# A decoder layer on one core: a prologue that runs shift and scale two block pairs ahead, an end without accumulating transfers, and side work visited by planned lag

## The chip, the core and the metric

The kernel runs on one core of a Trainium2 chip. The metric is the device time of one execution in microseconds (us). Engine names are those of the profile: PE is the tensor engine (PEld its weight loads), DVE the vector engine, ACT the scalar engine, POOL the GpSimd engine, and SP the queue from which most transfers are issued.

## What is computed

One layer of a decoder trunk for 1024 prompt tokens and 32 sample tokens (8 sequences of 4), model width 1024. The reference, cut to what matters:

```python
mod = silu(c) @ w_ada + b_ada                      # c: one row for the prompt, one per sample sequence
sh1, sc1, gt1, sh2, sc2, gt2 = split(mod, 6)
h = rmsnorm(x, g_pre_mix) * (1 + sc1) + sh1
z = h @ w_in                                       # 24 blocks of 128 columns
ya = chunk_gmlp(z...); yb = hgrn2(z...); yc = conformer_conv(z...)
y = concat(ya, yb, yc) @ w_out
x = x + gt1 * rmsnorm(y, g_post_mix)
h = rmsnorm(x, g_pre_mlp) * (1 + sc2) + sh2
y = square(relu(h @ w_up)) @ w_down
x = x + gt2 * rmsnorm(y, g_post_mlp)
```

Everything is float32. Large products are made from three products of a faster 32-bit matmul type: each operand is split into a rounded high part (`hi`) and the rest (`lo`), and hi·hi + hi·lo + lo·hi is accumulated.

## The kernel before

**Tiling.** Features lie on the 128 partitions. The 1056 tokens are cut into three token groups c = 0, 1, 2 of 352; the last 32 tokens of group 2 are the samples, whose shift and scale differ by sequence. The 1024 input features are 8 blocks k, kept in three tiles per group (blocks 0-2, 3-5, 6-7: the table `KK`). One output block of one group is 8 blocks x 3 matmuls of 128x128 by 128x352, summed in one PSUM bank.

**Prologue (lines 148-690).** The inputs `x` are loaded, squared on ACT (`first_squares`), folded over the blocks on DVE (`fold_first`), summed over the partitions on PE (`token_sums`), and turned into 1/rms per token (`token_rms`, `diagonal`, `by_feature`, `rstd_copy`). `scale_x` multiplies x by it, partly on DVE and partly on POOL. Shift and scale (`mod`, `G1`) come from `w_ada`, two blocks k at a time: 4 transfers (`ada_load`), 32 small matmuls (`ada_first`), a copy (`ada_copy`), and a transpose with the bias added (`ada_turn`). `first_h` makes hi and lo of h for one block and all groups. `first_blocks` goes over k and adds the products of the first two output blocks m = 0, 1 of all three groups in six banks; for a pair of blocks k it makes h, then issues the products, and between them the shift and scale of the next pair. `warm` issues matmuls of zeros. Behind the loop both blocks are evacuated, and the main part begins with the next output block (`in_block`).

**Main part.** Products follow a fixed order (`ORDER`, then `w_out`, `w_up`, `w_down`). Everything else (convolution taps on DVE, the recurrence, norms, the remaining shift and scale in `ada(q)`) is written as generators. `step(t)`, called between groups of matmuls, advances a planner's clock and visits generators whose due time has come while the planned load of the engines (`credit`) allows. A `yield 9.0` puts the next visit at least 9 planned us later. The visits decide only where instructions stand in each engine's queue; on the chip every engine goes through its queue in order.

**Norm between the halves.** `after_mix` (line 1361) scales one group, adds the input by an accumulating transfer from POOL's queue, stores the sum (`x1d`), waits 6.0, squares, sums and normalises again, and makes hi and lo for `w_up`.

**End.** The last product `w_down` goes over token groups `GROUPS`: group 2; then group 0 with 96 tokens of group 1; then the last 256 tokens of group 1. Behind each, `after_ff` (line 1475) scales by 1/rms. For the first two, `x1d` is added by accumulating transfers from POOL's queue and `out_yT` is then written from SP's; of the second, the last tile's part (kk = 2) is put off until the last group's sums are out. For the last group, `x1` lies in SBUF and DVE adds it.

Of the kernel before, what the change touches and what calls it, by code (L numbers as in the profile page):

```python
# [37 lines left out]
class Metered:  # L38
# [5 lines left out]
    def __getattr__(self, op):  # L44
        f = getattr(self._eng, op)

        def call(**kw):
# [5 lines left out]
            return f(**kw)  # L53

        return call
# [38 lines left out]
def trunk_kernel(ctx: ExitStack, tc: tile.TileContext, xT, cT, wada0, wada, vec, cst, msk, win, wout, wup,  # L94
# [245 lines left out]
    def ada(q):  # L340
        ps = bank("adaps")

        for k in range(8):
# [2 lines left out]
            raws = [e("rawada") for h2 in range(2)]
            for h2 in range(2):
                SP.dma_start(out=raws[h2][:, 0:1024], in_=wada[q - 1, k, h2])
            yield 7.0
            for j in range(4):  # L350
                PE.matmul(out=ps[32 * j:32 * j + 32, :], lhsT=scT[:, k, :],
                          rhs=raws[j // 2][:, (j % 2) * 512:(j % 2) * 512 + 512],
                          start=(k == 0), stop=(k == 7), skip_group_check=True)
            drop(2)
# [195 lines left out]
    def load_first(b):  # L550

        a = ada_load(b)
        rows = {0: slice(0, 2), 2: slice(2, 4), 4: slice(4, 8)}.get(b)
        if rows:
            for src, raw in raw_first:
                SP.dma_start(out=raw[:, rows, :], in_=src[:, rows, :])
        return a, rows
# [9 lines left out]
    x_s = mp.tile([128, 8, NS], F32, tag="s0", name="x_s")

    def first_squares(c):
        for kk, (k0, n) in enumerate(KK):  # L570
            ACT.activation(out=sqs[c][:, k0:k0 + n, :], in_=xs_in[c](kk), func=AF.Square)

    def fold_first(c, part):
        sq = sqs[c]
        for a, b, n in (((0, 3, 3),), ((0, 1, 1), (0, 2, 1), (6, 7, 1), (0, 6, 1)))[part]:
            DVE.tensor_tensor(out=sq[:, a:a + n, :], in0=sq[:, a:a + n, :], in1=sq[:, b:b + n, :], op=ALU.add)

    def rstd_copy(c, d):
        ps = by_feature(d)
        ACT.copy(out=rstds[c], in_=ps)  # L580

    def scale_x(c, eng, kk, a, b):

        w = CW if c < 2 else CW - NS
        t = xs_in[c](kk)[:, a:b, 0:w]
        eng.tensor_tensor(out=t, in0=t, in1=rep(rstds[c][:, 0:w], b - a), op=ALU.mult)

    G1 = cp.tile([128, 8, 9], F32, name="G1")
    for c in range(2):
        first_squares(c)  # L590
        fold_first(c, 0)
        fold_first(c, 1)
# [21 lines left out]
    scale_x(0, DVE, 0, 0, 2)
    fold_first(2, 1)
    rstd_copy(1, dg1)
    scale_x(1, POOL, 0, 2, 3)
    scale_x(1, POOL, 1, 0, 3)
    scale_x(1, DVE, 0, 0, 2)
    warm(3)  # L620
    (raw_ada, rows0) = ada_raws.pop(0)
    ada_0 = ada_first(raw_ada, 4)
    for i in range(2):
        next(ada_0)
    sums2 = token_sums(sqs[2][:, 0, :])
    rt2 = token_rms(sums2)
    dg2 = diagonal(rt2)
    next(ada_0)
    copied = ada_copy(next(ada_0))
    rstd_copy(2, dg2)  # L630
# [2 lines left out]
    warm(4)
    for kk, (k0, n) in enumerate(KK):
        POOL.tensor_copy(out=x_s[:, k0:k0 + n, :], in_=xs_in[2](kk)[:, :, CW - NS:])
    POOL.tensor_tensor(out=x_s, in0=x_s, in1=rep(rstds[2][:, CW - NS:], 8), op=ALU.mult)
    scale_x(2, POOL, 0, 2, 3)
    scale_x(2, POOL, 1, 0, 3)
    for c in range(NCH):
        scale_x(c, POOL, 2, 0, 2)  # L640
    h = [(hc(f"h{c}hi"), hc(f"h{c}lo")) for c in range(NCH)]
    sh1 = mod[:, 0:8, :]

    def first_h(k, cs=range(NCH)):

        ops = []
        for c in cs:
            w = CW if c < 2 else CW - NS
            u = xs_in[c](k // 3)[:, k % 3, 0:w]
            hi, lo = h[c][0][:, k, 0:w], h[c][1][:, k, 0:w]  # L650
            DVE.tensor_scalar(out=u, in0=u, scalar1=G1[:, k, 0:1], scalar2=sh1[:, k, 0:1], op0=ALU.mult, op1=ALU.add)
            ACT.copy(out=r(hi), in_=u)
            ops.append((u, hi, lo))
        for u, hi, lo in ops:
            DVE.tensor_tensor(out=r(lo), in0=u, in1=hi, op=ALU.subtract)

    def first_h_sample(k, n):

        u = x_s[:, k:k + n, :]
        hi, lo = h[2][0][:, k:k + n, CW - NS:], h[2][1][:, k:k + n, CW - NS:]  # L660
        DVE.tensor_tensor(out=b4(u), in0=b4(u), in1=seqs(G1[:, k:k + n, :]), op=ALU.mult)
        DVE.tensor_tensor(out=b4(u), in0=b4(u), in1=seqs(sh1[:, k:k + n, :]), op=ALU.add)
        ACT.copy(out=r(hi), in_=u)
        DVE.tensor_tensor(out=r(lo), in0=u, in1=hi, op=ALU.subtract)

    def first_blocks(evacs):

        pss = [[pm_tile() for c in range(NCH)], [pb.tile([128, CW], F32, tag="b", name="pmt2") for c in range(NCH)]]

        def products(k, c):  # L670
            xh, xl = (x[:, k, :] for x in h[c])
            for part, x in ((0, xh), (1, xh), (0, xl)):
                for m in range(2):
                    nc.tensor.matmul(out=pss[m][c], lhsT=r(w_first[m][part][:, k, :]), rhs=r(x),  # L674
                                     start=(k == 0 and part == 0 and x is xh), stop=(k == 7 and x is xl))

        for k in range(0, 8, 2):
            if k == 0:
                first_h(0, (0, 1))
                scale_x(2, DVE, 0, 0, 2)  # L680
                first_h(0, (2,))
            else:
                first_h(k)
            first_h_sample(k, 2)
            first_h(k + 1)
            if ada_raws and ada_raws[0][1]:
                split_first(ada_raws[0][1])
            for c in range(NCH):
                products(k, c)
            if k < 6:  # L690
                copied = ada_copy(next(ada_first(ada_raws.pop(0)[0])))
            if k < 4:
                ada_raws.append(load_first(k + 4))
            products(k + 1, 0)
            if k < 6:
                ada_turn(copied)
            products(k + 1, 1)
            products(k + 1, 2)
# [973 lines left out]
```

## Time and profile before

| | us |
|---|---|
| median of 3 runs (lowest, highest) | 1289.9 (1286.49, 1290.26) |
| the profiled execution, its own time | 1287.62 |
| its span, first to last instruction | 1285.9 |
| PE busy | 1239.1 (96%) |
| DVE busy | 743.7 (58%) |
| ACT busy | 474.4 (37%) |
| POOL busy | 112.7 (9%) |

The granted PE clock over the span is 0.981 of full. A row of a timeline or of the chain of waits gives start, duration and instruction; "x3" at its end merges three instructions; in brackets stands the idle time ahead of it and what ended it. A row of groups gives busy time, mean ns of one, and the idle time ahead. Rows of windows give busy time and count for PE, PEld, DVE, ACT and POOL, then the granted clock, the busy share of the transfer engines, and GB/s. Most operations are recorded on one helper line (L53), so groups are told apart by tiles.

### The profile page before, as it was taken

The numbers are of one execution on the slowest core, as the hardware profiler recorded it, in microseconds if no ns is written. First come the engines' busy times: TensorE is split into PE (matmuls) and PEld (weight loads), VectorE is DVE, ScalarE is ACT, GpSimd is POOL, SyncE is SP. The second block draws the span as 40 slices with busy tenths as digits, with TensorE's granted clock in tenths as the row PEclk, the third lists the DMA queues.
The fourth block names the chain that finished last, engine by engine and source line by source line (L and its number), as shares of the span: only waits on it lengthen the run. The fifth ranks groups of instructions, "written<-read, shape, count | busy, mean of one in ns | idle before, by whom it ended". The sixth has DMA issues, their size and how long they took to land.

```text
span 1285.9 us, 20903 instructions
## 1 busy us (share of the span) xinstructions
PE 1239.1 (96%) x8794; PEld 1196.8 (93%) x8794; DVE 743.7 (58%) x1206; ACT 474.4 (37%) x890; POOL 112.7 (9%) x135
## 2 busy tenths in 40 slices
PE   7799999999999999999999999999999999999994
PEld 6688898889999989999999999999999999999994
DVE  6888889986768758864333333333333333333365
ACT  4332464536674655655320320321311311312343
POOL 3300020302110133210000000000000000000002
PEclk7799999999999999999999999999999999999997
DMA  8446324310111364443211111111111111111218
GB/s 321 148 169 188 108 93 164 108 42 18 63 43 55 119 201 121 151 124 118 79 50 50 47 38 48 50 50 49 35 49 50 50 38 45 50 50 41 71 24 214
DMA packets 39376, 113.41 MB, mean 88 GB/s; under 512 B 10209, under 2 KB 12161, under 8 KB 39153
## 3 DMA queue, kind: packets, MB, share of 16 engines
q1 hardware_dynamic: 34544, 98.92, 22.5%
q0 software_dynamic: 4736, 13.14, 4.5%
q8 instruction: 69, 1.13, 0.3%
q14 instruction: 27, 0.21, 0.0%
HBM read 101.91 MB, written 10.14 MB: 87 GB/s over the span
## 4 chain that ended last, share of the span: by engine, by line
PE 86%; DVE 6%; ACT 3%; DMA 2%; issue 1%; POOL 1%; SPq 0%; ACTq 0%; DVEq 0%
PE pmt L53 78%; PE pmt L674 2%; PE adaps L53 2%; DVE sq L53 1%; PE sc L53 1%; DVE acc L53 1%; DMA rawada<-in_wada 1%; DMA o<-in_xT 1%; PE us L53 1%; DVE o L53 1%; PE stps L53 1%; PE ob L53 1%; DMA x<-in_xT 1%; ACT sq L53 1%; DVE x L53 0%
## 5 line engine op out<-in xcount | busy, mean ns | idle before, releaser
L53 PE MATMUL pmt<-ah,whi 128*128 128x352 f32 (+2 forms) x744 | 241.3, 324 | 0.8 <-ACT acc L53 0.8
L53 PE MATMUL pmt<-al,whi 128*128 128x352 f32 (+2 forms) x744 | 240.4, 323 | 0.3 <-DVE al L53 0.2
L53 PE MATMUL pmt<-ah,wlo 128*128 128x352 f32 (+2 forms) x744 | 240.3, 323 | 0.0
L53 ACT CAST whi<-raw 128x1024 fp32r<-128x1024 f32 (+2 forms) x114 | 115.2, 1014 | 261.9 <-PE pmt L53 259.4
L53 DVE TENSOR_TENSOR acc<-acc,pmt 128x352 f32<-128x352 f32 (+2 forms) x176 | 87.8, 502 | 167.9 <-PE pmt L53 167.9
L53 DVE TENSOR_TENSOR wlo<-raw,whi 128x1024 fp32r<-128x1024 f32 (+2 forms) x114 | 139.5, 1227 | 58.4 <-ACT whi L53 57.8
L53 DVE TENSOR_TENSOR rsq<-relu 128x352 f32<-128x352 f32 x84 | 44.1, 525 | 189.2 <-ACT relu L53 189.2
L53 PEld LDWEIGHTS pmt<-ah,whi 128*128 128x128 f32 x744 | 139.8, 188 | 2.2 <-ACT acc L53 1.0
L53 PEld LDWEIGHTS pmt<-al,whi 128*128 128x128 f32 x744 | 140.1, 188 | 1.6 <-DVE al L53 0.8
L53 PEld LDWEIGHTS pmt<-ah,wlo 128*128 128x128 f32 x744 | 139.9, 188 | 0.4
L53 ACT ACTIVATE relu<-pmt 128x352 f32<-128x352 f32 x96 | 44.5, 464 | 234.8 <-PE pmt L53 234.8
L53 PE MATMUL pmt<-h22hi,wlo 128*128 128x352 f32 x256 | 82.6, 323 | 0.0
L53 PE MATMUL pmt<-h22hi,whi 128*128 128x352 f32 x256 | 82.5, 322 | 0.0
L53 PE MATMUL pmt<-h22lo,whi 128*128 128x352 f32 x256 | 82.4, 322 | 0.0
L53 DVE SCALAR_TENSOR_TENSOR cva<-cvx,vec_t,cva 128x1024 f32<-128x1024 f32 x60 | 76.5, 1276 | 0.0
L53 PE MATMUL pmt<-h21hi,whi 128*128 128x352 f32 x232 | 75.1, 324 | 0.0
L53 PE MATMUL pmt<-h21hi,wlo 128*128 128x352 f32 x232 | 74.9, 323 | 0.0
L53 PE MATMUL pmt<-h20hi,wlo 128*128 128x352 f32 x232 | 74.9, 323 | 0.0
L53 PE MATMUL pmt<-h20hi,whi 128*128 128x352 f32 x232 | 74.8, 322 | 0.0
L53 PE MATMUL pmt<-h20lo,whi 128*128 128x352 f32 x232 | 74.7, 322 | 0.0
L53 PE MATMUL pmt<-h21lo,whi 128*128 128x352 f32 x232 | 74.7, 322 | 0.0
L1482 POOL DMA_DIRECT2D acc<-x1d x3 | 2.6, 877 | 699.6 <-DVE acc L53 689.5
(352 smaller groups left out, 2800.2 us busy)
## 6 DMA issues: line engine op xcount, KB each, us to landing
rawada<-in_wada SPq DMA_DIRECT2D x48, 512.0 KB, 6.2
raw<-in_wup SPq DMA_DIRECT2D x36, 512.0 KB, 3.4
raw<-in_wdn SPq DMA_DIRECT2D x36, 512.0 KB, 3.4
raw<-in_win SPq DMA_DIRECT2D x22, 512.0 KB, 3.6
raw<-in_wout SPq DMA_DIRECT2D x20, 512.0 KB, 3.6
x<-in_xT SPq DMA_DIRECT2D x6, 528.0 KB, 7.2
o<-in_xT POOLq DMA_DIRECT2D x6, 528.0 KB, 6.1
x1d<-o POOLq DMA_DIRECT2D x6, 528.0 KB, 7.3
```

The source lines that it names most:

```text
L53: return f(**kw)
L674: nc.tensor.matmul(out=pss[m][c], lhsT=r(w_first[m][part][:, k, :]), rhs=r(x), start=(k == 0 and part == 0 and x is xh), stop=(k == 7 and ...
L1482: POOL.dma_start(out=src(kk), in_=x1d[2][:, k0:k0 + n, :], accum_op=ALU.add)
```

## The change

1. **Prologue.** `x` is loaded in the order of groups 2, 0, 1. The constants one, epsilon and zero are set on POOL instead of loaded. Squares are no longer folded: PE multiplies each squared block by a matrix of ones, so that the sum appears on all partitions (21 matmuls of 352 columns; of group 1 DVE first adds one pair per tile), and 1/rms is one square root and one reciprocal of 128x352. POOL does no arithmetic on x. For groups 0 and 1 one DVE instruction applies 1/rms and scale, ACT adds the shift while it rounds hi, and DVE forms lo; for group 2 DVE applies 1/rms ahead (`scale_x`), and ACT scale and shift. Shift and scale of the first two pairs are made before the first product, h of pair p+1 during the products of pair p, and those of pair p+2 behind the products of its first block. The products of the last block k = 7 are issued per output bank, each followed by its evacuation. The weights of the next output block get a place of their own (`homes[2]`) and are split inside the loop.
2. **Paced visits.** Seven waits of generators change: five become `settle(extra, engines)`, a fixed part plus the planned backlog of the named engines (POOL is now planned too); `after_mix` waits 14.0 instead of 6.0; `ada(q)` takes two blocks at a time and waits 11.0 instead of 7.0 for one.
3. **End.** The tile kk = 2 of group 0 (with its 96 tokens of group 1) is no longer added by accumulating transfers: `x1d` of group 0, blocks 6-7, is loaded to SBUF (`x1_last`) and DVE adds both parts. The other accumulating transfers stay.

The diff, cut:

```diff
-    warm(30)
-    sums = [token_sums(sqs[0][:, 0, :])]
...
-    scale_x(0, POOL, 0, 2, 3)
-    scale_x(0, POOL, 1, 0, 3)
...
+    def first_squares(c, kk, added):
...
+        ACT.activation(out=sq[:, k0:k0 + n, :], in_=xs_in[c](kk), func=AF.Square)
+        if added:
+            DVE.tensor_tensor(out=sq[:, k0, :], in0=sq[:, k0, :], in1=sq[:, k0 + 1, :], op=ALU.add)
+        for k in range(k0, k0 + n):
+            if not added or k != k0 + 1:
+                PE.matmul(out=sums[c], lhsT=ones, rhs=sq[:, k, :], start=k == 0, stop=k == (6 if added else 7))
+
+    def first_rstd(c):
+        ACT.activation(out=rstds[c], in_=sums.pop(c), func=AF.Sqrt, scale=1.0 / 1024, bias=eps)
+        DVE.reciprocal(out=rstds[c], in_=rstds[c])
...
+        def plain(c):
+            ts = [(xs_in[c](kk)[:, a + i, :], k + i) for kk, a, b, k in spans(p) for i in range(b - a)]
+            for t, k in ts:
+                DVE.scalar_tensor_tensor(out=t, in0=t, scalar=G1[:, k, 0:1], in1=rstds[c], op0=ALU.mult,
+                                         op1=ALU.mult)
+                ACT.activation(out=r(h[c][0][:, k, :]), in_=t, func=AF.Identity, bias=sh1[:, k, 0:1], scale=1.0)
+            for t, k in ts:
+                DVE.scalar_tensor_tensor(out=r(h[c][1][:, k, :]), in0=t, scalar=sh1[:, k, 0:1],
+                                         in1=h[c][0][:, k, :], op0=ALU.add, op1=ALU.subtract)
...
+        plain(0)
+        last()
+        plain(1)
+        last_lo()
...
+    for i in range(3):
+        next(parts)
+        warm(2)
...
+    ada_turn(copied)
...
+    first_h(0)
+    scale_x(2, 1)
+    for at in ada_first(ada_raws.pop(0)):
+        warm(2)
+    copied = [ada_copy(at)]
+    ada_raws.append(ada_load(6))
...
+        for p in range(4):
+            k = 2 * p
+            both(0, k)
+            if p < 3:
+                ada_turn(copied.pop())
+                first_h(p + 1)
+                if p < 2:
+                    scale_x(2, p + 2)
+                    split_first(slice(2 * p + 2, (4, 8)[p]))
+                else:
+                    split_next()
             else:
...
+                ACT.copy(out=r(means), in_=cst_t[:, K_BLK:K_BLK + 256])
+            both(2, k)
+            both(1, k)
+            if p < 2:
+                for at in ada_first(ada_raws.pop(0)):
+                    pass
+                copied.append(ada_copy(at))
+            if p < 3:
+                for c in (0, 2, 1):
+                    both(c, k + 1)
...
+    def settle(extra, *keys):
+
+        return extra + max(0.0, *(-credit[k] for k in keys))
...
-        yield 9.0
+        yield settle(5.0, "act", "pool")
...
-        yield 3.0
+        yield settle(3.0, "act", "pool")
         drop()
         add_task("norm" if p < 3 else "last", head_norm(p, st, oo, sq, hi, lo))
...
-        yield 6.0
+        yield 14.0
         for d in sum_squares(src, box):
...
-                if last:
-                    DVE.tensor_tensor(out=y, in0=y, in1=x1[:, k0:k0 + n, a:b], op=ALU.add)
+                if kk < 2 and not last:
+                    POOL.dma_start(out=y, in_=x1d[c][:, k0:k0 + n, a:b], accum_op=ALU.add)
+                    SP.dma_start(out=yT[c, :, k0:k0 + n, a:b], in_=y)
                 else:
-                    POOL.dma_start(out=y, in_=x1d[c][:, k0:k0 + n, a:b], accum_op=ALU.add)
+                    rest.append((y, c, k0, n, a, b))
```

Where the instructions stand, at three places. First PE's queue behind the fillers (`pmt<-d`, products of zeros). `adaps` are the small matmuls of shift and scale for one pair, `adapt` the transpose that releases it, `h0hi` the high part of h of group 0. Before:

```order
L53 MATMUL pmt<-d_83 128x128 x3
L53 MATMUL adaps<-rawada,scT 32x128 x16
L53 MATMUL sums<-cst_t,sq_151 88x1 x4
L53 MATMUL adaps<-rawada,scT 32x128 x16
L53 MATMUL stps<-diag,cst_t 128x352
L53 MATMUL adapt<-cst_t,adasb 128x128
L53 MATMUL pmt<-d_83 128x128 x4
L674 MATMUL pmt<-h0hi,whi 128x352
```

After, from the first pair's transpose on:

```order
L56 MATMUL adapt<-cst_t,adasb 128x128
L56 MATMUL adaps<-rawada,scT 32x128 x8
L56 MATMUL pmt<-d_83 128x128 x2
L56 MATMUL adaps<-rawada,scT 32x128 x8
L56 MATMUL pmt<-d_83 128x128 x2
L56 MATMUL adaps<-rawada,scT 32x128 x8
L56 MATMUL pmt<-d_83 128x128 x2
L56 MATMUL adaps<-rawada,scT 32x128 x8
L56 MATMUL pmt<-d_83 128x128 x2
L673 MATMUL pmt<-h0hi,whi 128x352
```

The round of the second pair, 32 matmuls with eight fillers between them, now stands ahead of the first product; the sums of squares (`sums` and `stps` before) are all further ahead.

Second, DVE's queue from the moment that scale (`G`) of the first pair is known; `x_0_129` is group 0's tile of blocks 0-2 in the change. Before:

```order
L53 TENSOR_TENSOR mod<-adapt,vec_t 128x2x18
L53 SCALAR_TENSOR_TENSOR G_156<-mod,vec_t 128x18
L53 TENSOR_TENSOR wlo<-raw,whi 128x256 x2
L53 TENSOR_SCALAR x_0_105<-x_0_105,G_156,mod 128x352
L53 TENSOR_SCALAR x_0_111<-x_0_111,G_156,mod 128x352
L53 TENSOR_TENSOR h0lo<-x_0_105,h0hi 128x352
L53 TENSOR_TENSOR h1lo<-x_0_111,h1hi 128x352
L53 TENSOR_TENSOR x_0_117<-x_0_117,rstd 128x2x320
```

After:

```order
L56 TENSOR_TENSOR mod<-adapt,vec_t 128x2x18
L56 SCALAR_TENSOR_TENSOR G_154<-mod,vec_t 128x18
L56 SCALAR_TENSOR_TENSOR x_1_131<-x_1_131,G_154,rstd 128x352 x2
L56 SCALAR_TENSOR_TENSOR h0lo<-x_1_131,mod,h0hi 128x352 x2
L56 TENSOR_TENSOR x_1_125<-x_1_125,G_154 128x2x32
L56 TENSOR_TENSOR x_1_125<-x_1_125,mod 128x2x32
L56 SCALAR_TENSOR_TENSOR x_1_137<-x_1_137,G_154,rstd 128x352 x2
L56 SCALAR_TENSOR_TENSOR h1lo<-x_1_137,mod,h1hi 128x352 x2
L56 TENSOR_TENSOR h2lo<-x_1_125,h2hi 128x704
L56 TENSOR_TENSOR x_2_127<-x_2_127,rstd 128x704
L56 TENSOR_TENSOR wlo<-raw,whi 128x512 x2
```

These are the third pair's rows: eight instructions of 352 for two groups, group 2's after them, and the weights' low parts (`wlo`) for the pair that follows at the very end.

Third, DVE's queue in the last microseconds (`x` is `x1`, `x1l` is `x1_last`). Before:

```order
L53 TENSOR_TENSOR acc<-acc,rstd 128x704
L53 TENSOR_TENSOR acc<-acc,rstd 128x2x96
L53 RECIPROCAL rt<-rt 64x4
L53 TENSOR_TENSOR diag<-cst_t,rt 64x256
L53 TENSOR_TENSOR acc<-acc,rstd 128x3x256
```

After:

```order
L56 TENSOR_TENSOR acc<-acc,rstd 128x704
L56 TENSOR_TENSOR acc<-acc,rstd 128x2x96
L56 RECIPROCAL rt<-rt 64x4
L56 TENSOR_TENSOR diag<-cst_t,rt 64x256
L56 TENSOR_TENSOR acc<-acc,x1l 128x704
L56 TENSOR_TENSOR acc<-acc,x_11266 128x2x96
L56 TENSOR_TENSOR acc<-acc,rstd 128x3x256
```

Two additions of DVE stand where two accumulating transfers stood in POOL's queue.

More of the change, by code (lines that the diff above doesn't have):

```diff
@@ L166, in step @@
             for kind, q in queues.items():
-                if q and due[kind] <= clock[0] and all(credit[k] > 0 for k in uses.get(kind, credit)):
+                if q and due[kind] <= clock[0] and all(credit[k] > 0 for k in uses.get(kind, ("dve", "act", "pe"))):
                     try:
@@ L180, in trunk_kernel @@
     zero = mp.tile([128, NT], F32, name="d1")
-    POOL.memset(zero, 0.0)
+    POOL.memset(zero[:, 0:128], 0.0)
     cst_t = cp.tile([128, K_N], F32, name="cst_t")
+    ident = cst_t[:, K_ID:K_ID + 128]
+    ones = cst_t[:, K_ONE:K_ONE + 128]
+    eps = cst_t[:, K_EPS:K_EPS + 1]
+    POOL.memset(ones, 1.0)
+    POOL.memset(eps, EPS)
+    POOL.memset(zero[:, 128:], 0.0)
     csT = mp.tile([128, 8, 32], F32, name="csT")
@@ L341, in ada @@
         ps = bank("adaps")
-        for k in range(8):
-            while not room(4):
+        for k in range(0, 8, 2):
+            while not room(6):
                 yield 2.0
[L346 to L354, printed above, removed]
+            raws = [[e("rawada") for h2 in range(2)] for i in range(2)]
+            for i in range(2):
+                for h2 in range(2):
+                    SP.dma_start(out=raws[i][h2][:, 0:1024], in_=wada[q - 1, k + i, h2])
+            yield 11.0
+            for i in range(2):
+                for j in range(4):
+                    PE.matmul(out=ps[32 * j:32 * j + 32, :], lhsT=scT[:, k + i, :],
+                              rhs=raws[i][j // 2][:, (j % 2) * 512:(j % 2) * 512 + 512],
+                              start=(k + i == 0), stop=(k + i == 7), skip_group_check=True)
+            drop(4)
             yield
@@ L548, in trunk_kernel, with load_rows @@
     w_first = [[wp.tile([128, 8, 128], F32, tag=f"w{x}", name=f"w{x}") for x in ("hi", "lo")] for m in range(2)]
[L550 to L557, printed above, removed]
+    homes[2] = e3
+    def load_rows(rows):
+        for src, raw in raw_first:
+            SP.dma_start(out=raw[:, rows, :], in_=src[:, rows, :])
     def split_first(rows):
@@ L562, in split_first @@
             DVE.tensor_tensor(out=r(lo[:, rows, :]), in0=raw[:, rows, :], in1=hi[:, rows, :], op=ALU.subtract)
-    ada_raws = [load_first(0), load_first(2)]
-    sqs = [hc(f"sq{c}") for c in range(NCH)]
-    rstds = [rs("rstd")[:, 0:CW] for c in range(NCH)]
[L567 to L592, printed above, removed]
+    xs_in = {c: load3(xT[c], f"x{c}_") for c in FIRST}
+    SP.dma_start(out=ident, in_=cst[:, K_ID:K_ID + 128])
+    ada_raws = [ada_load(0)]
+    load_rows(slice(0, 2))
+    ada_raws.append(ada_load(2))
+    load_rows(slice(2, 4))
+    G1 = cp.tile([128, 8, 9], F32, name="G1")
+    sh1 = mod[:, 0:8, :]
+    rstds = [rs("rstd")[:, 0:CW] for c in range(NCH)]
     wps = pm_tile()
@@ L614, in trunk_kernel @@
[L614 to L630, printed above, removed]
-    ada_turn(copied)
-    split_first(rows0)
@@ L633, in trunk_kernel @@
[L633 to L681, printed above, removed]
-            else:
[L683 to L698, printed above, removed]
@@ new lines, in trunk_kernel, with first_product, both @@
+    pss = {}
+    def first_product(c, k, m, i):
+        if k == i == 0:
+            pss[m, c] = pb.tile([128, CW], F32, tag="b", name="pmt2") if m else pm_tile()
+        nc.tensor.matmul(out=pss[m, c], lhsT=r(w_first[m][i % 2][:, k, :]), rhs=r(h[c][i // 2][:, k, :]),
+                         start=k == i == 0, stop=k == 7 and i == 2)
+    def both(c, k):
+        for m, i in ((0, 0), (0, 1), (1, 0), (1, 1), (0, 2), (1, 2)):
+            first_product(c, k, m, i)
+    warm(14)
+    for i, c in enumerate(FIRST):
+        for kk in range(3):
+            first_squares(c, kk, i == 2)
+            if i == 1 and kk == 0:
+                first_rstd(2)
+                scale_x(2, 0)
+        if i == 0:
+            nc.scalar.preload_act_table(AF.Sqrt)
@@ new lines, in trunk_kernel @@
+    first_rstd(0)
+    parts = ada_first(ada_raws.pop(0))
+    for i in range(3):
+        next(parts)
+        warm(2)
+    first_rstd(1)
+    nc.scalar.preload_act_table(AF.Sigmoid)
+    split_first(slice(0, 2))
+    copied = ada_copy(next(parts))
+    ada_raws.append(ada_load(4))
+    load_rows(slice(4, 8))
+    warm(2)
+    ada_turn(copied)
+    first_h(0)
+    scale_x(2, 1)
+    for at in ada_first(ada_raws.pop(0)):
+        warm(2)
+    copied = [ada_copy(at)]
+    ada_raws.append(ada_load(6))
@@ L783, in conv_blocks @@
     def conv_blocks(j):
+        if not j:
+            first_blocks()
         sg, x = e(f"cvsg{j}"), e(f"cvx{j}")
@@ L1504, in after_ff @@
         d = diagonal(rt)
-        if not last:
+        if last:
+            add_rest()
+        else:
             yield 1.4
```

105 lines of the change are left out of this document (74 added, 31 removed).

## The prediction

> **What bounds the kernel now.** I read the windows first, cut where the kernel changes its nature: the prologue up to about 79 us, the mixer and the norms between the halves up to 600, the feed-forward part, and the end behind the last large product.
>
> ```profile
> 0.00:79.00 79.00, 59.62 (x533) 52.58 (x534) 57.22 (x110) 33.87 (x65) 22.59 (x28) 0.83 0.57 206
> 79.00:600.00 521.00, 510.68 (x4101) 479.13 (x4102) 413.35 (x641) 274.18 (x527) 80.92 (x98) 0.99 0.35 111
> 600.00:1262.00 662.00, 661.43 (x4106) 658.51 (x4104) 260.23 (x434) 161.43 (x287) 2.63 (x3) 1.00 0.16 51
> 1262.00:1286.00 24.00, 7.41 (x60) 6.53 (x58) 12.95 (x23) 4.92 (x14) 6.54 (x6) 0.71 0.93 225
> ```
>
> From 79 to 1262 us PE is busy but for 10.3 + 0.6 us, and the change leaves its products alone. So only three sums can move: the prologue, those 10.3 us, and the 24 us of the end. I then read the chain of waits and the timeline of the prologue, PE's waits over the whole run, and the timeline of the end.
>
> **The prologue: where its 79 us go.** Rows of the timeline up to the middle of the first pair, then of the chain of waits (window 45 to 80):
>
> ```profile
> 32.84 0.18 DVE L53 SCALAR_TENSOR_TENSOR G<-mod,vec_t 128x18 f32<-128x18 f32 x1
> 33.68 8.65 POOL L586 TENSOR_TENSOR x<-x,rstd 128x320 f32<-128x320 f32 x5
> 34.92 4.08 DVE L53 TENSOR_SCALAR x<-x,G,mod 128x352 f32<-128x352 f32 x2
> 37.83 0.96 PE L674 MATMUL pmt<-h0hi,whi 128*128 128x352 f32 x2 [4.14 <-ACT h0hi L53]
> 38.92 1.99 DVE L53 TENSOR_TENSOR h0lo<-x,h0hi 128x352 fp32r<-128x352 f32 x1
> 47.19 0.52 DVE L53 TENSOR_TENSOR h0lo<-x,h0hi 128x352 fp32r<-128x352 f32 x1
> ...
> 52.17 4.90 PE pmt L674 x30
> 57.07 1.88 PE adaps L53 x64
> 68.26 7.89 PE pmt L674 x47
> 78.87 1.23 PE pmt L53 x6
> ```
>
> The same DVE instruction takes 1.99 us while POOL works on x and 0.52 us after it has ended. Thirty products take 4.90 us, 0.163 each; a pair is 36 of them and a shift-and-scale round of 1.88, some 8 us, and from 51 us on PE runs at that pace. Ahead of it the first product waits until 37.83 for h. The main part begins at 78.87.
>
> **The prologue after the change.** The prices, from groups of instructions, the timeline and the chain:
>
> ```profile
> 15.06 2.72 ACT L53 ACTIVATE sq<-x 128x1056 f32<-128x1056 f32 x3
> 1239.39 0.59 PE stps L53 x2
> L53 DVE RECIPROCAL rstd<-rstd 128x352 f32<-128x352 f32 x1 | 2.4, 2353 | 1.8 <-ACT rstd L53 1.8
> 13.47 2.48 PE L53 MATMUL pmt<-d 128*128 128x128 f32 x20
> L53 ACT CAST h0hi<-x 128x352 fp32r<-128x352 f32 x8 | 3.9, 487 | 12.1 <-DVE x L53 12.1
> L53 ACT COPY adasb<-adaps 128x128 f32<-128x128 f32 x4 | 1.1, 266 | 6.0 <-PE adaps L53 6.0
> L53 PE MATMUL adapt<-cst_t,adasb 128*128 128x128 f32 x4 | 1.2, 309 | 0.0
> L53 DVE TENSOR_TENSOR mod<-adapt,vec_t 128x36 f32<-128x36 f32 x4 | 0.8, 195 | 7.9 <-PE adapt L53 7.9
> L53 DVE SCALAR_TENSOR_TENSOR acc<-acc,Go,rstd 128x320 f32<-128x320 f32 x8 | 4.0, 545 | 0.0
> L53 DVE TENSOR_TENSOR x<-x,rstd 128x704 f32<-128x704 f32 x2 | 1.8, 913 | 0.0
> L53 DVE TENSOR_TENSOR x_s<-x_s,G 128x64 f32<-128x64 f32 x4 | 0.9, 216 | 0.0
> L53 DVE TENSOR_TENSOR wlo<-raw,whi 128x512 fp32r<-128x512 f32 x2 | 1.3, 690 | 0.0
> L53 DVE TENSOR_TENSOR wlo<-raw,whi 128x256 fp32r<-128x256 f32 x2 | 0.8, 414 | 0.0
> ```
>
> *Up to the first scale.* The loads set ACT's squares, which end at 17.8 (15.06 + 2.72) before and about there after. A sum of squares is now a product of 352 columns, two rows and 0.59 us; 21 of them are 12.4 us of PE. The last five wait for DVE's additions behind the last squares and for the queue ahead; I put their end at 20.3. Then a round of shift and scale, 1.88, with six fillers (20 rows in 2.48, so 0.25 each): 3.4, to 23.7. Copy 0.27, transpose 0.31, `mod` 0.20, `G` 0.18, with hand-overs: `G` at 25.0 instead of 33.0. The reciprocals of 2.35 us lie beside PE's sums; the last ends at about 23.2, 1.8 us ahead of need.
>
> *The first product.* h0hi needs one DVE instruction (0.54) and one of ACT (0.49): 26.1. But PE's queue holds the second pair's round with eight fillers ahead of it, 1.88 + 2.0 from 24.6 on: the first product starts at 28.5, against 37.83.
>
> *The pairs.* DVE's work for one pair, with POOL silent: eight instructions of 352 at 0.54 (a little over the 0.50 of 320 columns), 4.3; samples 2 x 0.22; h2lo of 704 and `scale_x` of 704, 0.9 each; `wlo` 0.8 or 1.3; `mod` and `G` 0.4: 7.7 to 8.3. PE needs 8.0. The order ties them: `wlo` of the next pair stands last in DVE's queue, PE can do one product of the new pair before it needs it, then five more and the transpose, about 1.0 us, and only then can DVE go on. So a pair takes about 9, and PE waits some 2 us at the start of the second and third. In steps: `G` at 25.0, 32.1, 41.0, 50.2; the last h2lo at 55.8; behind it eight products, 1.3, and the 18 of k = 7, 2.9: 60.0. The next block's weights are split (1.2 of DVE) by 57, so it starts at 60.0, not 78.87: **-18.9**. The lower end is PE without a wait from 28.5: 144 products, two rounds and three transposes, 28, to 56.5, -22. The upper end is a PE at half clock, below: 65, -14. Transfers cover this: x, three rounds of shift and scale and the first weights are 11.4 MB by the page's sizes, and the rate of 410 GB/s in the row below puts the third round's last byte at about 31 us, when PE asks at 32.
>
> ```profile
> 10.00:20.00 10.00, 5.62 (x46) 4.83 (x46) 9.37 (x16) 7.63 (x11) 1.57 (x2) 0.96 1.03 410
> ```
>
> **The paced visits.** PE's waits between 79 and 600 us, nearly all of its 10.3 idle ones:
>
> ```profile
> PE stps L53 <- DVE sq L53: 4.3, 2, 4.1
> PE gnps L53 <- POOL gnlo L1165: 2.1, 1, 2.1
> PE adapt L53 <- ACT adasb L53: 1.9, 1, 1.9
> PE adaps L53 <- DMA rawada<-in_wada: 1.3, 2, 1.0
> ```
>
> Each has its counterpart: 14.0 for 6.0 ahead of `sq`, POOL's backlog for `gnlo`, ACT's and PE's for `adasb`, 11.0 for 7.0 for the loads. Together 9.6 us. What comes late instead: with 8 planned us more per group, the last third of group 1's h2 stands right ahead of its first `w_up` product. PE reaches it after 18 products, 2.9 us; DVE and ACT need 4 x 0.54 and two rounded parts of 0.49, 3.1, and a backlog of about one more: a new wait of about 1.5. Places that wait less than before (the convolution's tail, the copy of shift and scale) may give some back, say 2. I take **-6**, with 0 and -9.6 as ends.
>
> **The end.** Rows of the timeline, SP's waits from 1262 on, and the issues with their time to landing:
>
> ```profile
> 1270.83 2.14 POOL L1498 DMA_DIRECT2D acc<-x1d  x2 [1.89 <-DVE rt L53]
> 1275.93 2.29 SPq L1499 DMA_DIRECT2D out_yT<-acc  x2
> 1276.78 0.69 DVE L53 TENSOR_TENSOR acc<-acc,x 128x512 f32<-128x512 f32 x1
> 1280.60 1.15 SPq L1499 DMA_DIRECT2D out_yT<-acc  x2
> SPq L1499 <- DMA acc<-x1d: 12.6, 6, 5.5
> out_yT<-acc SPq DMA_DIRECT2D x1, 256.0 KB, 3.6
> ```
>
> DVE is done at 1277.5, but SP's queue stands behind two accumulating transfers issued at 1270.83 and writes the last output at about 1281.3; it lands and the span ends at 1285.9. After: the two additions of DVE (704 and 192 columns, about 1.2) fit between `diag` and the last 1/rms, where DVE waits that long for PE and ACT. SP still stands behind the four earlier accumulations; the last of them let it go at 1275.93. Then it issues five outputs, the last at 1278.1; with 3.6 to land, 1281.7, and the close of the span: **-3.5**. The ends are -1 (the transfer engines, busy for 0.93 of these 24 us, finish little sooner) and -5.
>
> **The sum.** 18.9 + 6 + 3.5 = 28.4. The profiled execution took 1287.62 with a span of 1285.9: 1259.2. The median shown, 1289.9, lies 2.3 above it and the lowest run 1.1 below; I say **1260**.
>
> **Rivals.**
>
> *PE falls to half clock between the pairs* (15%). The clock in the prologue:
>
> ```profile
> 36.00:37.00 1.00, 0.00 (x0) 0.00 (x0) 1.00 (x1) 0.00 (x0) 1.00 (x1) 0.66 0.00 0
> 39.00:50.00 11.00, 7.16 (x56) 5.70 (x58) 9.20 (x17) 3.03 (x8) 5.16 (x11) 0.50 0.01 2
> ```
>
> Ahead of the first product, at 37.83, PE stood still for 4.14 us, so from 33.7; the clock fell in the slice from 36 (0.66), so some 2.6 us in, and stayed at 0.50 to 50. My two waits of 2 us are just short of that. Each fall would cost about 2.5 (four us of products at half speed, and the rise): 1260 + 5 = **1265**. [...]
>
> *The visits only move the waits* (10%): the change does not do what it says there. Each of the four waits returns elsewhere as PE's queue is as strict as before: 1287.6 - 22.4 = **1265 to 1266**, to 1273 if the prologue is short as well.
>
> *Everything fits* (10%): PE at its own pace from 28.5, all 9.6 us gone, -5 at the end: **1251**.
>
> *Slower: DVE's slow instructions were not POOL's doing* (3%). The change gives DVE 32 instructions of 352 columns in `first_h`; at the 1.99 us of the row at 38.92 each is 1.45 over my price, 46 us on the path, **1306**. It ends slower by over 0.3% from about 1.0 us extra each (32 against 28.4 + 3.9). For it: I infer the sharing from one run. Against it: transfers, the other candidate, were at a share of 0.01 in 39 to 50, and the row at 47.19 is fast once POOL's stretch has ended.
>
> *The early start is lost again* (3%): DVE is busy 413 of 521 us in the mixer; if it were the bound there, PE would only wait later, about **1286**. Against it: DVE's work starts earlier by the same 19 us.
>
> **Chances.** The forecast, 1253 to 1266, has 59%. The range 1248 to 1273 takes in the half clock, the moved waits and most of the case where everything fits. 0.3%, 3.9 us, is about what a measurement of this kernel can tell from no change. Faster by more than that 0.94, within 0.03, slower 0.03.
>
> **What would show it.** Right: `G` of the first pair at 25, the first product near 28.5, `wlo` of 512 as what PE waits for in the third pair, the main part from 60; no DVE instruction of 352 columns over 0.6 us; PE idle below 5 us from there to the feed-forward part, with a short wait for h21lo; SP's last output right behind DVE's last addition. Wrong: a clock of 0.5 after 30 us, `rawada` as what PE waits for, new waits of `gnps` or `cmu`, or transfers that end as late as before.

## The result and the profile after

| | us | ratio to before (95% interval) |
|---|---|---|
| before, median of 10 runs | 1290.3 | |
| after, median of 10 runs (lowest, highest) | 1280.27 (1277.05, 1286.04) | 0.9928 (0.9909 to 0.9946) |
| the profiled execution of after, span 1284.2 | 1286.04 | |

The change gains 0.7%, some 9 us, where 30 were forecast. The windows of the profiled execution after the change, cut where the kernel changes its nature (length; busy time of PE, PE's weight loads, DVE, ACT and POOL; granted clock; share of the transfer engines; GB/s):

```profile
0.00:63.00 63.00, 59.28 (x507) 48.81 (x508) 40.76 (x81) 38.08 (x63) 3.40 (x18) 0.97 0.74 268
63.00:440.00 377.00, 368.40 (x3230) 342.48 (x3229) 314.37 (x511) 193.49 (x380) 50.77 (x66) 0.99 0.29 96
440.00:500.00 60.00, 58.54 (x360) 57.33 (x359) 38.50 (x37) 31.59 (x52) 18.80 (x21) 1.00 0.67 187
500.00:550.00 50.00, 39.21 (x205) 36.64 (x205) 35.56 (x53) 23.27 (x44) 9.86 (x10) 0.86 0.32 90
550.00:600.00 50.00, 50.00 (x313) 49.79 (x312) 25.93 (x45) 27.67 (x54) 1.10 (x2) 1.00 0.33 105
600.00:1262.00 662.00, 661.43 (x4108) 658.39 (x4107) 260.75 (x434) 162.10 (x287) 2.63 (x3) 1.00 0.17 52
1262.00:1285.00 23.00, 7.08 (x59) 6.38 (x57) 14.01 (x25) 4.60 (x13) 4.40 (x4) 0.74 0.86 214
```

The prologue did shrink: the main part begins at 63.09 instead of 78.87 (rows below). But in one stretch of 50 us, at the change from `w_out` to `w_up`, PE is busy for only 39.21 at a mean clock of 0.86. The same piece of work in the profile of before, some 16 us later, is full:

```profile
515.00:565.00 50.00, 49.81 (x309) 49.10 (x309) 38.60 (x55) 30.04 (x56) 11.29 (x12) 1.00 0.53 163
```

That execution lies 6 above its median, so the same kernel was run and profiled once more (after_again, span 1277.8). PE's waits over this whole run, longest first (what it waited for; us in total, times, longest). `gnps`, `ob` and `vf` belong to the recurrence (`vf` is a copy that ACT makes), `adapt` is the transpose of shift and scale, h21lo and h21hi are the second group's operands of `w_up`:

```profile
PE stps L56 <- DVE tot L56: 7.4, 2, 7.0
...
PE adapt L56 <- ACT adasb L56: 2.7, 1, 2.7
PE ob L56 <- ACT vf L56: 2.2, 2, 2.0
PE gnps L56 <- ACT vf L56: 2.1, 1, 2.1
...
PE pmt L56 <- DVE h21lo L56: 2.0, 1, 2.0
...
PE pmt L56 <- ACT h21hi L56: 1.0, 1, 1.0
```

The first row is new: 7.0 us for `tot`, the sum of squares of the third token group of `w_out`. This wait and those for h21lo and h21hi lie in the stretch of 50 us, and all three are new; the others lie in the mixer. There `gnps` and `adapt` are still waited for, `ob` is new, and the wait of 1.3 for the loads of shift and scale (`adaps`) is gone.

**What the order says of it.** PE's order after the change, from within the first `w_up` product (pmt of h20; whome is a part of its weight):

```
MATMUL pmt_5367<-h20hi_5162,whome_5192 128x352
MATMUL stps_5386<-tot_5027,cst_t_85 128x352
MATMUL pmt_5367<-h20hi_5162,whome_5191 128x352
MATMUL pmt_5367<-h20lo_5163,whome_5191 128x352
MATMUL pmt_5367<-h20hi_5162,whome_5192 128x352
MATMUL pmt_5367<-h20hi_5162,whome_5191 128x352
MATMUL pmt_5367<-h20lo_5163,whome_5191 128x352
MATMUL pmt_5367<-h20hi_5162,whome_5192 128x352
MATMUL stps_5403<-sq_5297,cst_t_85 128x352
```

Before, the sum of `sq` (second group) stood in the last `w_out` product, and that of `tot` in the first product of h21, with the four products of h20 between them:

```
MATMUL pmt_5395<-yh2_4652,whome_4693 128x352
MATMUL stps_5414<-sq_5317,cst_t_85 128x352
MATMUL pmt_5395<-yh2_4652,whome_4692 128x352
...
MATMUL pmt_5600<-h21hi_5429,wlo_5386 128x352
MATMUL stps_5607<-tot_5115,cst_t_85 128x352
MATMUL pmt_5600<-h21hi_5429,whi_5385 128x352
```

So the second group's sum now stands behind the third group's, and the third's stands four products earlier than before. By the code, the third group's generator waits only 2.5 ahead of its sum, so it goes first while the second group's waits for its 14.0. ACT and DVE in after_again, at that place (start, duration, instruction; in brackets the idle time ahead and what ended it):

```profile
501.34 2.73 ACT L56 ACTIVATE sq<-o 128x1056 f32<-128x1056 f32 x3
505.04 1.23 DVE L56 TENSOR_TENSOR wlo<-raw,whi 128x1024 fp32r<-128x1024 f32 x1 [3.05 <-ACT whi L56]
506.18 4.03 DVE L56 TENSOR_TENSOR sq<-sq 128x1056 f32<-128x1056 f32 x4
510.12 1.07 DVE L56 SCALAR_TENSOR_TENSOR h20lo<-o,mod,h20hi 128x352 fp32r<-128x352 f32 x2
511.12 0.52 DVE L56 TENSOR_TENSOR tot<-tot,sqb 128x352 f32<-128x352 f32 x1
```

`tot` is the last of DVE's four rows, behind 4.03 us of folding the second group's squares, and PE's queue stands until it is done. The same squares hold ACT for 2.73 us ahead of `whi`, for which DVE waits 3.05. The first group's last h2 (`h20lo`) stands behind them as well. Before, it stood ahead of them:

```profile
510.13 1.08 DVE L53 SCALAR_TENSOR_TENSOR h20lo<-o,mod,h20hi 128x352 fp32r<-128x352 f32 x2 [0.16 <-ACT h20hi L53]
515.88 5.27 DVE L53 TENSOR_TENSOR sq<-sq 128x1056 f32<-128x1056 f32 x4 [1.44 <-ACT sq L53]
```

### The profile page after: what moved, and what is told of

Read it like the earlier page. It is cut to its first block, busy times and chain, and to the rows that moved or that the text cites. A ratio compares the mean times of both kernels' runs of the same rounds, so it can differ in the third digit from the quotient of the medians.

```text
span 1284.2 us, 20789 instructions
## 1 busy us (share of the span) xinstructions
PE 1243.9 (97%) x8770; PEld 1199.8 (93%) x8770; DVE 729.9 (57%) x1182; ACT 480.8 (37%) x890; POOL 91.0 (7%) x123
## 4 chain that ended last, share of the span: by engine, by line
PE 81%; DVE 8%; ACT 6%; issue 2%; DMA 2%; POOL 1%; SPq 0%; DVEq 0%; ACTq 0%; POOLq 0%
PE pmt L56 74%; PE adaps L56 1%; PE stps L56 1%; DVE acc L56 1%; DMA raw<-in_wup 1%; DMA o<-in_xT 1%; PE sc L56 1%; DVE wlo L56 1%; DVE o L56 1%; PE pmt L673 1%; DVE sq L56 1%; ACT sq L56 1%; ACT whi L56 1%; DVE R L56 1%; DVE q L56 1%
## 5 line engine op out<-in xcount | busy, mean ns | idle before, releaser
L56 DVE TENSOR_TENSOR wlo<-raw,whi 128x1024 fp32r<-128x1024 f32 (+2 forms) x113 | 136.5, 1210 | 70.0 <-ACT whi L56 69.9
L56 DVE TENSOR_TENSOR al<-rsq,ah 128x352 fp32r<-128x352 f32 x96 | 50.4, 525 | 26.9 <-ACT ah L56 17.8
```

## The experiments

All ratios are to the kernel before, timed beside it on the same chip (its median beside the experiments was 1288.2 to 1289.0). A difference between two ratios is given in us of some 1288. "Idle" and "half clock" are worked out from windows of 2 us from 58 to 620 us of each profile: idle sums 2 less the busy time of PE over the windows where it is busy for less than 1.9, or the clock is not full; half clock sums (1 less the granted clock) x 2. The two overlap where PE stands still at half clock, so they are not to be added up.

| run | what it is | median us | ratio (interval) | idle | half clock |
|---|---|---|---|---|---|
| before | | 1290.3 | 1 | 12.5 | 3.4 |
| pro_only | before + prologue | 1269.14 | 0.9846 (0.9830 to 0.9863) | 8.7 | 1.7 |
| end_only | before + end | 1286.15 | 0.9980 (0.9970 to 0.9991) | 12.6 | 5.1 |
| vis_only | before + visits | 1294.53 | 1.0040 (1.0027 to 1.0053) | 18.5 | 8.5 |
| pro_end | before + prologue + end | 1267.49 | 0.9829 (0.9811 to 0.9847) | 8.5 | 3.4 |
| pe_w14 | pro_end + the 14.0 | 1277.35 | 0.9904 (0.9890 to 0.9918) | 15.6 | 8.5 |
| pe_set | pro_end + five settle values | 1274.5 | 0.9884 (0.9867 to 0.9901) | 11.1 | 3.4 |
| pe_conv | pro_end + two of them | 1272.3 | 0.9871 (0.9856 to 0.9886) | 10.2 | 5.1 |
| pe_ada | pro_end + loads in twos | 1271.7 | 0.9865 (0.9849 to 0.9881) | 11.6 | 6.8 |
| w6 | after without the 14.0 | 1271.15 | 0.9861 (0.9847 to 0.9875) | 11.0 | 8.5 |
| after_again | after | 1279.78 | 0.9929 (0.9916 to 0.9941) | 17.9 | 10.2 |
| after_tot | after, tot's sum later | 1278.26 | 0.9914 (0.9900 to 0.9929) | 16.5 | 8.5 |
| after_x1d | after, stores of x1 later | 1279.16 | 0.9921 (0.9907 to 0.9935) | 19.0 | 12.0 |
| after_warm | after + fillers | 1276.4 | 0.9901 (0.9886 to 0.9916) | 11.5 | 3.4 |
| pe_w10_6 | pro_end, 10.0 for group 0 | 1269.57 | 0.9853 (0.9839 to 0.9867) | 8.7 | 3.4 |
| pe_x1d | pro_end, stores of x1 later | 1266.97 | 0.9823 (0.9808 to 0.9838) | 7.5 | 1.7 |

### The three parts apart

w6 is the changed kernel with one line undone:

```diff
-        yield 14.0
+        yield 6.0
         for d in sum_squares(src, box):
```

> The changed kernel with 6.0 in place of 14.0 ahead of the squares in after_mix, all else as changed. Theory A (the 14.0 puts h2 of the first two groups and the sum of the third group behind work that PE then waits for, at 505 to 545 us): the waits of 7.1 for tot, 2.5 and 1.0 for h21 go, the clock stays full there, a wait for sq of up to 4 returns; 1280.3 - 11 + 0 to 4 = 1269 to 1273, ratio to the kernel before 0.984 to 0.987. Theory B (the early start is eaten in the mixer by the other visits, whatever stands here): within 2 of the changed kernel, 1278 to 1282, ratio 0.991 to 0.994.

Measured: 0.9861, 8.6 under the changed kernel. The wait for `tot` is gone, a wait of 3.2 for `sq` is back. Theory B would have left it at 0.991 or more.

pro_only, vis_only and end_only are the kernel before with one of the three parts of the diff each.

> The kernel before with the new prologue alone (old visits, old end). Theory A: the prologue is worth what its trace shows, 15 to 16, and nothing behind it takes it back; 1290 - 15.5 = 1274 to 1275, ratio 0.988. Theory B (PE catches up with something in the mixer that doesn't start earlier): 1280 to 1288, ratio 0.992 to 0.998.

> The kernel before with the paced visits alone (old prologue, old end). Theory A: they cost about 11 around the third group of w_out and save some 4 to 6 in the mixer; 1290 + 5 to 8 = 1295 to 1298, ratio 1.004 to 1.006. The prediction on record (visits are worth -6): 1284, ratio 0.995.

> The kernel before with the new end alone. The prediction on record: -3.5, 1286.5, ratio 0.9973. What the two traces show from DVE's last addition to the end of the span (8.4 before, 7.0 after): -1.4, 1288.7, ratio 0.9989.

Measured: -19.8, +5.2 and -2.6 (each is the ratio less 1, times some 1288). The early start is not lost: the prologue alone is worth more than either theory of pro_only gave it. The end lies between its two expectations. The visits alone make the kernel slower, as theory A has it, with the same wait at the same place as in the changed kernel; PE's waits of vis_only between 495 and 560:

```profile
PE stps L56 <- DVE tot L56: 7.0, 1, 7.0
PE pmt L56 <- DVE h21lo L56: 2.2, 1, 2.2
PE pmt L56 <- ACT h21hi L56: 1.0, 1, 1.0
```

pro_end has the prologue and the end, and the old visits.

> New prologue and new end, old visits. If parts add up: 0.9846 x 0.998 = 0.9826, some 22 under the kernel before. If the end's gain hangs on what stands ahead: 0.9846. If it is below 0.985, the visits are shown to cost the changed kernel (0.9928) at least 10.

Measured: 0.9829. Prologue and end add up (0.9846 x 0.998 = 0.9826). What is left, from 0.9829 to 0.9928, 12.8 us, is what the visits cost the changed kernel.

### Which visit costs what

Each of these is pro_end and one group of the new values. pe_w14 has the 14.0 alone:

> New prologue and new end, and of the visits only 14.0 in place of 6.0 ahead of the squares, for all three groups. Theory A (the 14.0 by itself puts h2 and the third group's sum behind work that PE waits for): 8 to 10 over pro_end, ratio 0.989 to 0.991. Rival (it costs that only together with the other visits, which shift the third group): 0.983 to 0.985.

Measured: 0.9904, 9.7 over pro_end: the 14.0 does it by itself (theory A). Its waits are 7.1 for `tot`, 2.3 for h21lo, 1.0 for h21hi.

pe_set has the five `settle` values, pe_conv the first two of them:

```diff
-        yield 9.0
+        yield settle(5.0, "act", "pool")
...
-        yield 6.0
+        yield settle(4.0, "act", "pool")
```

> New prologue and new end, and of the visits only the five settle values of the mixer (old loads of shift and scale, 6.0 ahead of the squares). w6 (0.9861) lies some 4.5 above the sum of prologue and end (0.9826). Theory A (the settle values cost it: waits of ob for vf of 2.0 in place of gnps for gnlo of 2.1, and half clock behind them): 0.985 to 0.986. Theory B (the loads in twos and the copy visited early cost it, adapt 2.7 for 1.0): 0.982 to 0.983.

> New prologue and new end, and of the settle values only the convolution's two. Theory A (the recurrence's three make ACT wait for DVE ahead of vf, which PE then waits for): 0.983, as without them. Theory B (the convolution's two do, by starting the recurrence in another place): 0.988, as with all five.

Measured: 0.9884, 7.1 over pro_end and dearer than both theories of pe_set, and 0.9871 with the convolution's two alone: most of it is theirs, so theory B of pe_conv holds. It isn't the wait that I named, though: `ob` costs pe_set 0.2. PE's waits of pe_set, window 190 to 330, and ACT's rows at that place:

```profile
PE gnps L56 <- ACT vf L56: 3.5, 1, 3.5
PE vtps L56 <- ACT vf L56: 1.0, 1, 1.0
```

```profile
308.00 0.45 ACT L56 COPY vf<-pmt 128x352 f32<-128x352 f32 x1 [0.54 <-PE pmt L56]
314.10 0.62 ACT L56 COPY KA<-K 128x512 f32<-128x512 f32 x1 [5.66 <-DVE K L56]
...
314.75 0.44 ACT L56 COPY vf<-pmt 128x352 f32<-128x352 f32 x1
317.90 0.62 ACT L56 COPY QS<-QB 128x512 f32<-128x512 f32 x1 [2.71 <-DVE QB L56]
```

ACT stands 5.66 and 2.71 for DVE, and copies (`vf`), which end PE's waits, are queued behind. In the order of pro_end PE waits 2.1 for `gnlo` (POOL) there and not for `vtps`. These rows account for some 2.4 of the 7.1 (idle 11.1 against 8.5 by the table); where the rest goes isn't shown.

pe_ada has the loads of shift and scale in twos and the early copy. Its wait is a sixth `settle` and an eighth changed wait, beside the seven that the section on the change counts:

```diff
-        yield 3.0
+        yield settle(1.5, "act", "pe")
         pt = pb.tile([128, 4, 128], F32, tag="b", name="adapt")
```

> New prologue and new end, and of the visits only the loads of shift and scale in twos with the copy visited early. By w6 against pe_set (0.9861 against 0.9884, which differ in these loads alone) they gain 3: 0.9806 from 0.9829. Rival (the two differ by the accidents of the settle values' order): 0.983 to 0.985, with adapt waited for 2.7 in place of 1.0.

Measured: 0.9865, 4.6 over pro_end: a loss where a gain of 3 was expected. The rival has the sign right (`adapt` at 2.7), but the loss is larger than its 0.983 to 0.985. PE's waits of pro_end, then of pe_ada, both from 190 to 330 us:

```profile
PE gnps L56 <- POOL gnlo L56: 2.1, 1, 2.1
PE adapt L56 <- ACT adasb L56: 1.0, 1, 1.0
```

```profile
PE adapt L56 <- ACT adasb L56: 2.7, 1, 2.7
PE ob L56 <- ACT vf L56: 2.2, 2, 2.0
PE gnps L56 <- ACT vf L56: 2.0, 1, 2.0
```

The single costs are 9.7, 7.1 and 4.6, but together 12.8, and settle and loads together (w6) 4.1. They do not add, by more than the intervals allow. The traces show a new order each time, with waits in other places.

### What makes the 7 us

after_tot moves the third group's sum behind the first `w_up` products:

```diff
-        yield 2.5
+        yield 16.0 if c == 2 else 2.5
         rstd = rstd_of(tot)
```

> The changed kernel, with the first visit of after_mix for the third group after 16.0 in place of 2.5, so that the sum of tot stands behind the first up products and not ahead of them. Theory A (the place of this sum in PE's queue makes the wait of 7.1): that wait goes, a wait of 2 to 3 for sq or h21 comes in part of its place, 5 to 8 gained: ratio 0.987 to 0.989. Theory B (h2 of the second group is late anyway and PE only waits for it there): 0.991 to 0.993.

Measured: 0.9914, no clear gain, as theory B has it. The wait for `tot` is gone, and PE waits instead for `h20lo`, which stands just ahead of `tot` in DVE's queue, behind the same folding of squares:

```profile
509.84 0.66 PE L56 MATMUL pmt<-h20lo,whome 128*128 128x352 f32 x1 [5.27 <-DVE h20lo L56]
529.92 0.43 PE L56 MATMUL pmt<-h21hi,whi 128*128 128x352 f32 x1 [1.74 <-ACT h21hi L56]
```

after_x1d moves POOL's stores of x1, which wait for the accumulating loads, behind the squares; pe_x1d does the same to pro_end:

```diff
-        for kk, (k0, n) in enumerate(KK):
-            POOL.dma_start(out=x1d[c, :, k0:k0 + n, :], in_=src(kk))
         yield 14.0
-        for d in sum_squares(src, box):
+        for i, d in enumerate(sum_squares(src, box)):
+            if i == 2:
+                for kk, (k0, n) in enumerate(KK):
+                    POOL.dma_start(out=x1d[c, :, k0:k0 + n, :], in_=src(kk))
             yield d
```

> The changed kernel with the three stores of x1 into x1d, which stand in POOL's queue ahead of the 14.0 and hold it until the accumulating loads have landed, behind the squares. Theory A (POOL, held by these stores, adds the third group's squares late and in a bunch beside DVE, and that is what makes tot 7 late): POOL's waits of 1.7 to 3.5 for o from in_xT go, the wait for tot falls under 3, 4 to 7 gained, ratio 0.9875 to 0.990. Theory B (the h2 of the second group, put off by 14.0, stands ahead of tot in DVE's queue whatever POOL does): within 0.15% of 0.9928.

> New prologue and new end, old visits, with the same move of the stores of x1 behind the squares. Theory A: the wait for sq of 3.5 at 461 us stays (it hangs on the accumulating loads), the rest is as good or better: 0.980 to 0.983. Rival (the stores then hold o when it is scaled in place, and h2 comes late): 0.984 or more.

Measured: 0.9921, theory B. POOL's waits for the accumulating loads are gone from its list (first after_again, then after_x1d, both 470 to 520), and PE still waits 7.0 for `tot`:

```profile
POOL x1d L1415 <- DMA o<-in_xT: 7.8, 3, 3.8
```

```profile
POOL tot L56 <- ACT sqb L56: 15.5, 5, 3.8
POOL o L1412 <- DVE o L56: 12.0, 2, 11.8
POOL o L1412 <- POOL o L56: 0.3, 1, 0.3
```

So POOL's stores do not make the 7 us, and putting the sum of `tot` later does not free PE by itself. What is left is the second group's squares ahead of `h20lo` and `tot` on ACT and DVE; without the 14.0 (w6) the wait is gone. pe_x1d, 0.9823, is where its theory A put it and the lowest of all, but its interval overlaps that of pro_end.

after_warm fills the two waits with products whose result is thrown away: 26 in front of the sum of `tot`, 10 in front of the first product of h21.

```diff
+    def fillers(ps, n):
+        for i in range(n):
+            nc.tensor.matmul(out=ps[:, 0:128], lhsT=ones, rhs=ident, start=True, stop=True)
...
+        fillers(ps, fill)
         PE.matmul(out=ps, lhsT=ones, rhs=tot, start=True, stop=True)
```

> The changed kernel with 26 filler products (6.5 us at full clock) ahead of the sum of tot and 10 (2.5) ahead of the first up product of the second group, where PE waits 7.1 and 2.5. Theory A (half clock behind these waits costs 4 to 6 beside the waits themselves): clock 1.00 from 505 to 550, 3 to 6 gained, ratio 0.988 to 0.9905. Theory B (only the waits count, DVE's and ACT's chain sets the time): within 0.1% of 0.9928.

> The changed kernel once more, unaltered, for a second profiled execution: the first (span 1284.2) lies 6 above its median of 1280.3. If the waits around the third group of w_out are its own doing and no accident, they are there again, 4 to 8 us of them for tot, h20lo or h21, with half clock behind; ratio 0.991 to 0.9945. If they were an accident of the first one: idle time there under 2.

Measured: after_warm 0.9901, after_again 0.9929: 3.6 gained by work that computes nothing, as theory A has it (the two intervals just meet). The windows 500 to 550 of after_again, then of after_warm:

```profile
500.00:550.00 50.00, 40.04 (x217) 37.73 (x216) 31.23 (x50) 23.90 (x47) 6.69 (x8) 0.86 0.36 94
```

```profile
500.00:550.00 50.00, 46.67 (x306) 45.12 (x305) 32.14 (x52) 26.03 (x50) 7.39 (x9) 1.00 0.37 100
```

pe_w10_6 tries the later visit where h2 has room, for the first group alone:

```diff
-        yield 6.0
+        yield 10.0 if c == 0 else 6.0
```

> New prologue and new end, old visits, with 10.0 in place of 6.0 ahead of the squares of the first group alone, whose h2 is needed last by 14 planned us. Theory A: the wait for sq of 3.5 at 461 us and the half clock behind it (1.7) go and nothing comes: 0.979 to 0.981. Rival (as with 14.0 for all: what is put off meets the third group's sum): 0.983 or more.

Measured: 0.9853, the rival: no gain, and if anything a loss. The one wait of 3.5 for `sq` became two (pro_end, then pe_w10_6, 440 to 520):

```profile
PE stps L56 <- DVE sq L56: 3.5, 1, 3.5
```

```profile
PE stps L56 <- DVE sq L56: 4.3, 2, 2.3
```

## Why the prediction was wrong, point by point

- **Prologue, -18.9: right as a sum, and that by luck.** The runs give -19.8 for it alone. The trace of the changed kernel gives 78.87 - 63.09 = 15.8 up to the main part, where all of the 18.9 was forecast. Most of the rest comes behind it, where pro_only has 3.8 less idle and 1.7 less half clock than before by the table (2.0 of that idle time is the tail of the old prologue, already in the 15.8). Nothing in the forecast stands for this gain, and no run shows what makes it. The pairs took longer than the 9 of the working:

```profile
25.29 0.18 DVE L56 SCALAR_TENSOR_TENSOR G<-mod,vec_t 128x18 f32<-128x18 f32 x1
29.64 0.41 PE L673 MATMUL pmt<-h0hi,whi 128*128 128x352 f32 x1
32.52 0.18 DVE L56 SCALAR_TENSOR_TENSOR G<-mod,vec_t 128x18 f32<-128x18 f32 x1
40.71 0.61 PE L673 MATMUL pmt<-h0hi,wlo 128*128 128x352 f32 x1 [1.93 <-DVE wlo L56]
42.98 0.18 DVE L56 SCALAR_TENSOR_TENSOR G<-mod,vec_t 128x18 f32<-128x18 f32 x1
47.32 1.08 DVE L56 SCALAR_TENSOR_TENSOR h1lo<-x,mod,h1hi 128x352 fp32r<-128x352 f32 x2 [0.42 <-ACT h1hi L56]
52.39 0.18 DVE L56 SCALAR_TENSOR_TENSOR G<-mod,vec_t 128x18 f32<-128x18 f32 x1
63.09 3.02 PE pmt L56 x19
```

  Step by step, forecast and found: first product 28.5 and 29.64; `G` 25.0, 32.1, 41.0, 50.2 and 25.29, 32.52, 42.98, 52.39; main part 60.0 and 63.09. PE's wait of about 2 for `wlo` came at the second pair, with the rival's half clock behind it (at the third it was 0.2):

```profile
40.00:44.00 4.00, 3.29 (x12) 3.22 (x13) 2.18 (x7) 0.19 (x1) 0.00 (x0) 0.60 0.06 19
```

  In after_again the same wait, 1.9, left the clock full (1.00 over 0 to 63), and the main part ran 0.9 ahead (its first product of `h1hi` with `whome` at 65.81 instead of 66.74): the fall cost some 0.9 there, not the rival's 2.5, which was an estimate. What I left out is DVE's own waiting for ACT inside a pair, 0.16 to 0.85 at each rounded part. With POOL silent two of DVE's instructions of 352 columns took 1.08, 0.54 each as priced, so the rival "DVE's slow instructions were not POOL's doing" falls.

- **Paced visits, -6: the step that failed.** Instead of gaining 6 they cost 12.8 beside the new prologue and end, and 5.2 alone. The prediction said of the four waits "Each has its counterpart" and booked their 9.6 us as gone, less 2 for places that wait less; it priced one new wait, h21, at 1.5. h21 came, at 2.0 + 1.0 in after_again, twice the price. The wait of 7.0 for `tot` I did not see; the 14.0 that brings it makes 8.6 to 9.7 of the loss (w6, pe_w14). I asked what is queued behind the instructions that the 14.0 delays for group 1, and not which sums and operands of the other groups PE then meets first. The swap, `tot` ahead of `sq`, could have been read from PE's order before any run. Of the waits counted as gone, `sq` (4.3) and the loads' `adaps` (1.3) went; `gnps` stayed at 2.1, now for `vf` on ACT, `adapt` rose from 1.9 to 2.7, and `ob` came with 2.2.

- **Half clock behind waits: counted in the prologue only.** The windows from 58 to 620 us give 3.4 us of it before and 10.2 to 11.9 after; nothing in the -6 stands for it. Filling the two waits brought 3.6 back.

- **The end, -3.5: right in kind, somewhat large.** -2.6 by the runs, with 1.2 to 3.9 by the interval. SP's rows after the change:

```profile
1276.62 0.38 SPq L1541 DMA_DIRECT2D out_yT<-acc  x1
...
1279.26 0.80 SPq L1549 DMA_DIRECT2D out_yT<-acc  x1
```

  Four of the last six accumulating transfers are still there, and the last of them let SP go at 1276.62, where I had put 1275.93, the time of the fourth before. DVE's last addition lies 0.3 earlier than before, so the fourth came a full 1.0 later; why it did with two fewer behind it isn't shown. The last output went at 1279.26 instead of 1278.1. In windows of 2 us the transfer engines are at a share of 1.00 to 1.29 from 1268 to 1282, which is what the prediction gave as a reason for a smaller gain.

- **Rivals.** "The visits only move the waits" was the nearest in mechanism, with 1265 to 1273 too low: some of the waits moved, and they grew. "The early start is lost again" (1286) came as near in time for a reason that the runs refute: pro_only keeps all of it.

- **What stays open.** Why the visits' costs do not add (9.7 + 7.1 + 4.6 against 12.8) is only read from the traces, as other orders with other waits; no run isolates it. None of the versions here has a paced visit that clearly pays.

## What to carry to other kernels

Where a planner places side work in strict queues, a wait value moves whole chains: read from the order what now stands ahead of what on the engine that bounds the kernel, for the neighbours of the moved step too, before booking the old wait as gone. Time the parts of a change apart: here one line of the visits gave back about 9 of the 22 us that prologue and end won, and prologue and end alone (0.9829) beat both kernels. On PE count a wait as its length and, where the clock falls behind it, as more: before, two falls, behind waits of 1.9 (`adapt`) and 4.1 (`sq`), make 1.7 of the 3.4 us of half clock each; the one behind 1.93 in the changed kernel's prologue set the main part back by some 0.9.

## What the runs showed of the hardware

Behind a wait of 2.07 us PE's clock was halved, behind one of 2.08 it was not. The two are the same wait for `gnlo` in two kernels, pro_end first, with the window behind it:

```profile
304.92 0.43 PE L56 MATMUL gnps<-gnlo,means 128*128 128x352 f32 x1 [2.07 <-POOL gnlo L56]
...
306.00:308.00 2.00, 2.00 (x9) 2.00 (x8) 1.89 (x2) 0.54 (x2) 0.65 (x2) 0.50 0.00 0
```

```profile
304.74 0.43 PE L56 MATMUL gnps<-gnlo,means 128*128 128x352 f32 x1 [2.08 <-POOL gnlo L56]
...
306.00:308.00 2.00, 2.00 (x13) 1.82 (x13) 2.00 (x2) 1.38 (x4) 0.57 (x1) 1.00 0.00 0
```

In pro_end the clock fell after work had begun again and came back between 308 and 310 (0.95 from 304 to 306, 0.70 from 308 to 310); in pe_x1d it stayed full (1.00 from 302 to 310). In the changed kernel's prologue it fell behind a wait of 1.93 (0.60 from 40 to 44); in after_again it stayed full behind the same wait of 1.9. Which of the two happens in a given execution may be a part of the spread of the changed kernel, 1277 to 1286 in ten runs against 1286 to 1292 before; that is a guess, which no run tries by itself.
